# A hybrid attention and gating layer: output weights and gating result kept in memory as high and low parts

## The chip, the cores and the metric

One core of a Trainium2 chip runs the whole layer. The metric is the device time of one launch in microseconds (us), as the median of several runs. The core's engines work side by side, each through its own queue in order: TensorE (PE, with its weight loads PEld), VectorE (DVE), ScalarE (ACT), GpSimd (POOL), and SyncE (SP), which here issues every DMA.

## What is computed

The input x (2048 tokens by 1024) goes through one projection. Eight attention heads and a gating unit use its result, both results are joined (1024 wide) and go through one output projection, and a layer norm with a scaled residual ends it. Cut to what matters here:

```python
proj = jnp.einsum('bsd,de->bse', h, w_in)
attn = _causal_attention(qf, kf, val).reshape(b, s, MLA_WIDTH)
out_a = attn * jax.nn.silu(z_a)
sgu = u * sv.reshape(b, s, G_WIDTH)          # u, v: gelu; sv: causal mix of v
out_b = sgu * jax.nn.silu(z_b)
merged = jnp.concatenate([out_a, out_b], axis=-1)
y = jnp.einsum('bse,ed->bsd', merged, w_out)
h = _layernorm(DN_ALPHA * h + y, ln_g, ln_b)
```

## The kernel before

**Precision.** A float32 product is made of three matmuls on numbers in the format fp32r. Each operand is split into a high part (ACT copies it into an fp32r tile) and a low part (DVE subtracts the high part from the operand); the product is high by high, high by low and low by high. So an operand that comes from memory costs a load into one of five `raw` buffers, one copy on ACT and one subtraction on DVE. All the subtractions go through a helper and carry its line, L98.

**Input stage** (up to some 515 us). Two halves of 1024 tokens. In each, blocks of features of `w_in` (c = 0 to 11, 128 columns each; `feat`) are multiplied for two tiles of 512 tokens (L859). Blocks 4 to 7 give u, so their gelu times the gate (ACT L970, POOL L978) is the gating result out_b, stored whole as `ob_d` (L992). After block 7 come the latents (L853), whose weights w_c go into ring slots 0 to 3 as soon as block 5 has left them. The activations of a gate block hold a `tmp` buffer, of which there are ten.

**Attention** (some 515 to 1050 us). Eight heads, each of four query tiles of 512, with 3, 7, 11 and 15 units: 36 units in a head. A unit is three score matmuls (L422 to L424), exponent and high part on ACT (L432, L438), the low part on DVE (`pl`, L98), a row sum on POOL (L453) and two matmuls with the values (L466, L467). Beside a head run the row maxima for the next (L349 on PE, L356 and L359 on DVE). A finished tile needs a fold on ACT and DVE, a sum on POOL, and in odd heads two products on POOL (L600) whose factors come over DMA: the tile's row sums are gathered (`lc`, L578), inverted, stored (`r_d`, L584), loaded broadcast (`rb`, L596), and the product is stored as `oa_d` (L606).

**Output projection.** Its operands are the eight blocks of `w_out` (k = 0 to 7) and, for each tile st of 512 tokens, eight blocks of the joined result: k = 0 to 3 from `oa_d`, k = 4 to 7 from `ob_d`. `weights` (L1398, L1401) loads and splits the 16 half blocks of weights, `merged` (L1413, L1416) the eight blocks of tile 0, all in heads 6 and 7. Tile 0 is then multiplied inside head 7 (`block`, eight of them, 24 matmuls each, L1381 into bank_c), tile 1 is loaded at the end of head 7, tiles 2 and 3 by `load_m` (L1367) while the tile before is multiplied (L1381 into bank_a).

**What sets the order.** `op` records each step with engine, length, rank and dependencies; `issue` plays them through with booked lengths (`LENGTH`, `LAG`; 2.4 us for the landing of a DMA) and writes each engine's queue in that order. Among steps that can start, the lowest rank wins; a step that could start earlier fills a gap. Two engines are kept apart (`pair`) where the step says so; the subtractions of `weights` and `merged` do not say it. `YSTART` and the `spread` calls at the end of `y_jobs` set the ranks of the output projection's steps in units.

## Time and profile before

| | before |
|---|---|
| median of 3 runs | 1188.37 us (1185.0 to 1190.04) |
| the profiled execution | 1188.45 us, its span 1186.4 us |
| PE busy | 1148.7 us of the span (97%) |
| DVE, ACT, POOL busy | 851.1, 614.8, 505.3 us |
| PE's share of the chain that ended last | 83% |
| moved by DMA | 117.09 MB |

The profile is of one execution. Busy time is a share over stages with different limits, so the stretches are read one by one: the input stage to about 515 us, heads 0 to 5 to 872.7 us, head 6 to 936.2 us, head 7 to about 1032 us, the rest of the output projection to the end. "Granted clock" (PEclk) is TensorE's clock as a share of full speed.

### The profile page before, as it was taken

The numbers are of one execution on the slowest core, as the hardware profiler recorded it, in microseconds if no ns is written. First come the engines' busy times: TensorE is split into PE (matmuls) and PEld (weight loads), VectorE is DVE, ScalarE is ACT, GpSimd is POOL, SyncE is SP. The second block draws the span as 40 slices with busy tenths as digits, with TensorE's granted clock in tenths as the row PEclk, the third lists the DMA queues.
The fourth block names the chain that finished last, engine by engine and source line by source line (L and its number), as shares of the span: only waits on it lengthen the run. The fifth ranks groups of instructions, "written<-read, shape, count | busy, mean of one in ns | idle before, by whom it ended". The sixth has DMA issues, their size and how long they took to land.

```text
span 1186.4 us, 17288 instructions
## 1 busy us (share of the span) xinstructions
PE 1148.7 (97%) x5497; PEld 942.0 (79%) x5497; DVE 851.1 (72%) x2022; ACT 614.8 (52%) x1203; POOL 505.3 (43%) x482
## 2 busy tenths in 40 slices
PE   8999999999999999999999999999999879999997
PEld 6888899878888997777777777877777558878886
DVE  4777455446743386568899889898989973459866
ACT  5552413246433124248888788887888663432000
POOL 1112210101022121118799989987999774510000
PEclk9999999999999999989999999999999889999999
DMA  7311414365124216330031112111322234276431
GB/s 248 97 54 46 137 39 147 110 200 164 41 59 117 80 49 194 131 112 28 27 90 55 45 48 70 54 46 40 79 77 72 72 89 142 80 224 229 160 133 63
DMA packets 76075, 117.09 MB, mean 99 GB/s; under 512 B 18304, under 2 KB 22416, under 8 KB 75792
## 3 DMA queue, kind: packets, MB, share of 16 engines
q1 hardware_dynamic: 75984, 115.99, 31.4%
q8 instruction: 43, 0.70, 0.3%
q14 instruction: 48, 0.39, 0.1%
HBM read 79.58 MB, written 36.24 MB: 98 GB/s over the span
## 4 chain that ended last, share of the span: by engine, by line
PE 83%; DVE 5%; DMA 4%; ACT 3%; POOL 3%; issue 2%; SPq 0%; DVEq 0%; POOLq 0%; ACTq 0%
PE bank_a L859 22%; PE bank_a L853 13%; PE bank_a L1381 11%; PE bank_c L349 5%; PE bank_a L422 4%; PE bank_b L467 4%; PE bank_b L466 4%; PE bank_a L423 4%; PE bank_a L424 4%; PE bank_c L1381 3%; PE bank_a L1186 2%; PE bank_b L930 2%; POOL acc L453 1%; DVE pl L98 1%; PE bank_c L311 1%
## 5 line engine op out<-in xcount | busy, mean ns | idle before, releaser
L859 PE MATMUL bank_a<-xbuf,ring 128*128 128x512 f32 x1152 | 278.8, 394 | 6.3 <-ACT xbuf L709 5.5
L859 PEld LDWEIGHTS bank_a<-xbuf,ring 128*128 128x128 f32 x1152 | 215.1, 189 | 51.0 <-ACT xbuf L709 6.1
L432 ACT ACTIVATE bank_a<-bank_a 128x512 f32<-128x512 f32 (+1 forms) x288 | 163.6, 575 | 82.2 <-PE bank_a L424 47.2
L453 POOL TENSOR_TENSOR acc<-acc,xbuf 128x512 f32<-128x512 f32 (+2 forms) x168 | 194.9, 1160 | 21.3 <-ACT xbuf L438 12.6
L853 PE MATMUL bank_a<-ring,xbuf 128*128 128x512 f32 (+1 forms) x768 | 169.9, 373 | 0.0
L853 PEld LDWEIGHTS bank_a<-ring,xbuf 128*128 128x128 f32 x768 | 142.9, 189 | 16.5
L98 DVE TENSOR_TENSOR ring<-raw,ring 128x512 fp32r<-128x512 f32 (+1 forms) x88 | 70.9, 816 | 100.2 <-ACT ring L709 92.7
L359 DVE TENSOR_REDUCE mxt<-bank_c 128x1 f32<-128x512 f32 (+1 forms) x192 | 126.9, 666 | 18.4 <-PE bank_c L349 16.6
L98 DVE TENSOR_TENSOR pl<-bank_a,xbuf 128x512 fp32r<-128x512 f32 (+1 forms) x192 | 125.9, 661 | 18.2 <-ACT xbuf L438 16.8
L467 PE MATMUL bank_b<-pl,xbuf 128*128 128x512 f32 (+1 forms) x320 | 119.2, 376 | 9.4 <-ACT bsb L528 6.4
L438 ACT CAST xbuf<-bank_a 128x512 fp32r<-128x512 f32 (+1 forms) x192 | 107.6, 574 | 7.6 <-ACT bank_a L432 0.4
L453 POOL TENSOR_TENSOR acc<-acc,ph 128x512 f32<-128x512 f32 (+1 forms) x72 | 86.0, 1195 | 11.4 <-ACT ph L438 7.4
L466 PE MATMUL bank_b<-xbuf 128*128 128x512 f32 (+2 forms) x216 | 81.3, 380 | 0.0
L467 PEld LDWEIGHTS bank_b<-pl,xbuf 128*128 128x128 f32 x320 | 61.8, 193 | 20.0 <-ACT bsb L528 6.9
L98 DVE TENSOR_TENSOR pl<-bank_a,ph 128x512 fp32r<-128x512 f32 x96 | 65.1, 685 | 16.6 <-ACT ph L438 15.9
L356 DVE CUSTOM_DVE_ANT_0 bank_c<-bank_c,maskq 128x256 f32<-128x256 f32 (+3 forms) x128 | 65.7, 519 | 8.0 <-PE bank_c L349 6.9
L709 ACT CAST ring<-raw 128x512 fp32r<-128x512 f32 (+1 forms) x72 | 42.2, 601 | 55.9 <-PE bank_a L859 31.7
L970 ACT ACTIVATE act_t<-bank_a 128x512 f32<-128x512 f32 x40 | 23.9, 598 | 85.5 <-PE bank_a L859 85.1
L422 PE MATMUL bank_a<-xbuf,ring 97*128 97x512 f32 (+2 forms) x160 | 61.7, 386 | 3.6 <-DVE pl L98 3.3
L98 POOL TENSOR_TENSOR held<-qrt 128x128 f32<-128x128 f32 x16 | 7.4, 460 | 133.2 <-DVE qrt L1144 123.5
L422 PE MATMUL bank_a<-q,ring 97*128 97x512 f32 (+2 forms) x160 | 62.3, 389 | 0.3 <-DVE pl L98 0.3
L349 PE MATMUL bank_c<-ring,xbuf 96*128 96x512 f32 (+2 forms) x160 | 60.9, 390 | 1.0 <-DVE mxt L359 0.6
...
## 6 DMA issues: line engine op xcount, KB each, us to landing
...
```

What stands on the lines that cost most here:

```text
L98: eng.tensor_tensor(out=out_, in0=a, in1=b, op=ALU.subtract)
L349: pe.matmul(st_["x"][:, :hi - lo], qs_(h, 0)[0:DQK, qb * P:end], kslot(h)[0:DQK, 0, lo:hi], start=True, stop=True)
L359: dve.tensor_reduce(out=mx[h][:, qb, c:c + 1], in_=xps, axis=AX.X, op=ALU.max)
L422: pe.matmul(o_, k_[0:DQK + 1, 0, js], q_[0][0:DQK + 1, qs], start=True, stop=False)
L432: act.activation(out=o_, in_=o_, func=AF.Exp, scale=SCALE)
L438: act.copy(out=un["ph"][:, c0:512], in_=un["x"][:, c0:512])
L453: pool.tensor_tensor(out=t_["acc"][:, cs], in0=t_["acc"][:, cs], in1=f(p_), op=ALU.add)
L466: pe.matmul(a_ps[:, cs], va, un["ph"][:, ps], start=first, stop=last)
L467: pe.matmul(b_ps[:, cs], vb, un["pl"][:, ps], start=first, stop=last and qt > 0)
L853: pe.matmul(dst[:, :n], a[:, k, js], b[:, 0:4, k, 0:cols], start=(k == 0 and i == 0), stop=(k == KT - 1 and i == 2))
L859: pe.matmul(dst, a[:, slot, k, :], b[:, k, :], start=(k == 0 and i == 0), stop=(k == KT - 1 and i == 2))
L1381: pe.matmul(y, mo(st, k, a)[:, js], wo(k, w)[:, ns], start=(k == kord(st)[0] and i == 0), stop=(k == kord(st)[-1] and i == 2))
```

## The change

The weights of the output projection are split in the input stage. While feature blocks 4 to 7 are multiplied, `keep_wo` loads a half block of `w_out`, copies its high part (ACT), subtracts (DVE) and stores both parts in the new `wo_d` (16 half blocks over the two halves). The gating result is split there too: `feat` copies its high part into a second `tmp` buffer, subtracts, and stores both parts in `ob_d`, which is now twice as large. In heads 6 and 7 `weights` is a plain transfer of 512 KB into the ring, `ckv` or `wo` tile for each block and part (16 of them), and `merged` for k = 4 to 7 two transfers of 256 KB. `load_m` does likewise for tiles 2 and 3. Blocks k = 0 to 3 are still split on arrival, their subtraction now kept apart from POOL's steps. `YSTART` goes from 6 to 14, and two ranges of ranks end later.

```diff
-    UNITS, YSTART, VLATE = 36, 6, 9
+    UNITS, YSTART, VLATE = 36, 14, 9
+    WO_AT = 4
-    ob_d = dram.tile([4, P, S], F32, name="ob_d")
+    ob_d = dram.tile([2, 4, P, S], F32, name="ob_d")
+    wo_d = dram.tile([2, KT, P, D], F32, name="wo_d")
...
+        def keep_wo(k, n, rank):
+            ns = slice(n * 512, (n + 1) * 512)
+            st_ = {}
+            def load():
+                st_["raw"] = raw2k([P, 512])
+                sp.dma_start(out=st_["raw"], in_=w_out[k * P:(k + 1) * P, ns])
+            def high():
+                st_["h"] = tp.tile([P, 512], F32R, name="wo_h", tag="held2k", bufs=2)
+                act.copy(out=st_["h"], in_=st_["raw"])
+            def store(c):
+                sp.dma_start(out=wo_d[c, k, :, ns], in_=st_["raw"] if c else f(st_["h"]))
+            d_ = op("sp", 256, rank, load)
+            h_ = op("act", 512, rank, high, [d_])
+            l_ = op("dve", 512, rank, lambda: sub(dve, st_["raw"].bitcast(F32R), st_["raw"], f(st_["h"])), [h_],
+                    times=1.1, pair=True)
+            s_ = [op("sp", 256, rank, lambda c=c: store(c), [o]) for c, o in enumerate((h_, l_))]
+            d_.takes.append(("raw", [s_[1]]))
+            h_.takes.append(("held", [s_[0], l_]))
...
-            if c >= 4:
-                dst = ob_d[c - 4, :, ss] if c < 8 else za_d[c - 8, :, ss]
-                o = op("sp", 256, rank, lambda: sp.dma_start(out=dst, in_=st_["t"]), [o])
+            if 4 <= c < 8:
+                h_ = op("act", 512, rank + 2, lambda: act.copy(out=st_["h"], in_=st_["t"]), [o])
+                l_ = op("dve", 512, rank + 2, lambda: sub(dve, st_["t"].bitcast(F32R), st_["t"], f(st_["h"])), [h_],
+                        times=1.1, pair=True)
+                s_ = op("sp", 256, rank + 2, lambda: sp.dma_start(out=ob_d[0, c - 4, :, ss], in_=f(st_["h"])), [h_])
+                o = op("sp", 256, rank + 2, lambda: sp.dma_start(out=ob_d[1, c - 4, :, ss], in_=st_["t"]), [l_])
+                a_.takes.append(("tmp", [s_, l_]))
...
+                    if WO_AT <= c < WO_AT + 4:
+                        keep_wo(4 * hf + c - WO_AT, s2, T)
...
+        if k > 3:
+            for c in range(2):
+                sp.dma_start(out=f(mo(st, k, c)), in_=ob_d[c, k - 4, :, ss])
+            return
...
-        def weights(k, n, r):
+        def weights(k, c, r):
...
             def load():
-                if k in (2, 3) and n == 0:
+                if k in (2, 3) and c == 0:
                     wo8_alloc(k - 2)
-                st_["raw"] = raw2k([P, 512])
-                sp.dma_start(out=st_["raw"], in_=w_out[k * P:(k + 1) * P, ns])
-            d_ = op("sp", 0, r, load, [done["s"][H - 2, 0 if k > 3 else NT - 1]])
-            h_ = op("act", 512, r, lambda: act.copy(out=wo(k, 0)[:, ns], in_=st_["raw"]), [d_, *(old if k > 3 else idle)])
-            l_ = op("dve", 512, r, lambda: sub(dve, wo(k, 1)[:, ns], st_["raw"], f(wo(k, 0)[:, ns])), [h_])
+                sp.dma_start(out=f(wo(k, c)), in_=wo_d[c, k])
+            ready.setdefault(k, []).append(op("sp", 512, r, load, old if k > 3 else idle))
...
+            def parts():
...
+                for c in range(2):
+                    sp.dma_start(out=f(mo(st, k, c)), in_=ob_d[c, k - 4, :, st * 512:(st + 1) * 512])
+            if k > 3:
+                ready.setdefault(k, []).append(op("sp", 512, r, parts, deps, times=1.2))
+                return
-            l_ = op("dve", 512, r, lambda: sub(dve, mo(st, k, 1), st_["raw"], f(mo(st, k, 0))), [h_])
+            l_ = op("dve", 512, r, lambda: sub(dve, mo(st, k, 1), st_["raw"], f(mo(st, k, 0))), [h_], pair=True)
...
-        for ks, lo, hi in ((KORD[:4], base - UNITS + 18, base), (KORD[4:], base + 2, base + 14)):
+        for ks, lo, hi in ((KORD[:4], base - UNITS + 18, base), (KORD[4:], base + 2, base + 24)):
...
-               base + YSTART + 6, base + UNITS + 6)
+               base + YSTART + 6, base + UNITS + 14)
```

Since `issue` writes the queues anew, three places matter.

**DVE, near the end of head 6.** `mxt` is the maximum over a row, `oa_9669` and `ckv` take a block of tile 0 and a block of weights. Before:

```order
L98 TENSOR_TENSOR pl<-bank_a,xbuf 128x512
L98 TENSOR_TENSOR oa_9669<-raw,oa_9669 128x512
L372 TENSOR_REDUCE mrow<-mxt 128x4
L98 TENSOR_TENSOR pl<-bank_a,xbuf 128x512
L98 TENSOR_TENSOR ckv<-raw,ckv 128x512
L98 TENSOR_TENSOR pl<-bank_a,xbuf 128x512
L359 TENSOR_REDUCE mxt<-bank_c 128x1
```

The same place now (the helper's line is L101 there):

```order
L101 TENSOR_TENSOR pl<-bank_a,xbuf 128x512
L375 TENSOR_REDUCE mrow<-mxt 128x4
L362 TENSOR_REDUCE mxt<-bank_c 128x1
L101 TENSOR_TENSOR pl<-bank_a,xbuf 128x512 x2
L362 TENSOR_REDUCE mxt<-bank_c 128x1
```

The two subtractions are gone, and nothing stands between the units' own.

**PE, in head 7, where tile 0 of the output projection begins.** Before, behind the scores of head 7's 22nd unit:

```order
L424 MATMUL bank_a<-xbuf,ring 128x512
L1381 MATMUL bank_c<-ring,xbuf 128x512 x3
L1381 MATMUL bank_c<-ring,oa_9669 128x512 x3
L1381 MATMUL bank_c<-ring,xbuf 128x512 x3
L1381 MATMUL bank_c<-ring,oa_9669 128x512 x3
L1381 MATMUL bank_c<-ckv,oa_9669 128x512 x12
L1381 MATMUL bank_c<-ring,xbuf 128x512 x12
```

Now, behind the scores of the 25th unit (L427 is the third of the score matmuls, L469 and L470 are those with the values):

```order
L427 MATMUL bank_a<-xbuf,ring 128x512
L469 MATMUL bank_b<-xbuf 128x256
L470 MATMUL bank_b<-pl,xbuf 128x256
L469 MATMUL bank_b<-xbuf 128x256
L470 MATMUL bank_b<-pl,xbuf 128x256
L1415 MATMUL bank_c<-ring,xbuf 128x512 x3
L1415 MATMUL bank_c<-ring,oa_9520 128x512 x3
L1415 MATMUL bank_c<-ring,xbuf 128x512 x3
L1415 MATMUL bank_c<-ring,oa_9520 128x512 x3
L1415 MATMUL bank_c<-ckv,oa_9520 128x512 x12
L1415 MATMUL bank_c<-ring,xbuf 128x512 x6
```

The projection starts three units later. Of its 192 matmuls 96 now stand behind the last scores of head 7, where 42 stood.

**SP, in the first half of the input stage, around the loads of w_c.** Before:

```order
L702 DMA raw<-in_w_feat_dram 128x512 x8
L702 DMA raw<-in_w_c_dram 128x416 x5
L992 DMA ob_d<-act_t 128x512 x2
L702 DMA raw<-in_w_c_dram 128x416 x3
```

Now, from the store of the second tile of feature block 5 on:

```order
L1024 DMA ob_d<-act_h 128x512
L1025 DMA ob_d<-act_t 128x512
L743 DMA wo_d<-raw 128x512
L705 DMA raw<-in_w_c_dram 128x416 x2
L736 DMA raw<-in_w_out_dram 128x512
L705 DMA raw<-in_w_c_dram 128x416
L1024 DMA ob_d<-act_h 128x512
L1025 DMA ob_d<-act_t 128x512
L743 DMA wo_d<-wo_h 128x512
L743 DMA wo_d<-raw 128x512
L705 DMA raw<-in_w_c_dram 128x416 x4
```

One store of a gating tile pair and one load of w_c follow these. The loads of w_c now stand behind stores that wait for ACT, POOL and DVE.

## Rows read from the trace of the kernel before

**Rows 1.** The page: busy time, share of the span and instructions by engine.
```profile
PE 1148.7 (97%) x5497; PEld 942.0 (79%) x5497; DVE 851.1 (72%) x2022; ACT 614.8 (52%) x1203; POOL 505.3 (43%) x482
```

**Rows 2.** Busy time by stretch: input stage, head 2, head 6, head 7, the rest.
```profile
core 0: us, PE busy (x) PEld busy (x) DVE busy (x) ACT busy (x) POOL busy (x), PEclk, DMA share, GB/s
96.00:156.00 60.00, 60.00 (x270) 50.24 (x269) 37.41 (x85) 20.30 (x35) 15.90 (x12) 1.00 0.30 92
342.00:402.00 60.00, 60.00 (x270) 50.36 (x269) 15.81 (x20) 18.21 (x33) 15.70 (x12) 1.00 0.29 86
...
636.60:693.70 57.10, 55.92 (x275) 44.14 (x274) 51.26 (x112) 45.87 (x88) 53.12 (x47) 1.00 0.19 52
872.70:936.20 63.50, 59.50 (x273) 45.01 (x272) 60.78 (x117) 51.71 (x103) 57.66 (x48) 0.95 0.30 84
936.20:981.00 44.80, 34.84 (x154) 25.62 (x153) 36.68 (x59) 31.55 (x62) 30.70 (x24) 0.92 0.32 89
981.00:1046.00 65.00, 65.00 (x293) 53.19 (x293) 26.70 (x41) 22.80 (x40) 31.42 (x26) 1.00 0.37 117
1046.00:1058.00 12.00, 9.77 (x40) 6.67 (x39) 4.86 (x9) 3.21 (x6) 1.14 (x1) 1.00 0.80 229
```

**Rows 3.** Groups of instructions, 872.7 to 981 us: busy us, mean ns | idle before.
```profile
L453 POOL TENSOR_TENSOR acc<-acc,xbuf 128x512 f32<-128x512 f32 (+2 forms) x33 | 40.6, 1230 | 3.5 <-ACT xbuf L438 1.7
...
L98 DVE TENSOR_TENSOR pl<-bank_a,xbuf 128x512 fp32r<-128x512 f32 (+1 forms) x38 | 24.8, 656 | 2.1 <-ACT xbuf L438 1.9
...
L98 DVE TENSOR_TENSOR ring<-raw,ring 128x512 fp32r<-128x512 f32 x8 | 9.3, 1164 | 0.0
...
L98 DVE TENSOR_TENSOR oa<-raw,oa 128x512 fp32r<-128x512 f32 x3 | 6.8, 2259 | 0.0
...
L1401 ACT CAST wo<-raw 128x512 fp32r<-128x512 f32 x4 | 2.5, 618 | 5.3 <-DMA raw<-in_w_out_dram 5.3
```

**Rows 4.** In order of time (start, us): a long subtraction, two stops of PE.
```profile
917.49 4.34 DVE L98 TENSOR_TENSOR oa<-raw,oa 128x512 fp32r<-128x512 f32 x1
...
949.54 0.50 PE L422 MATMUL bank_a<-xbuf,ring 97*128 97x512 f32 x1 [2.28 <-DVE pl L98]
...
971.20 0.80 PE L467 MATMUL bank_b<-pl,xbuf 128*128 128x512 f32 x1 [6.43 <-ACT bsb L528]
```

**Rows 5.** Chain that ended last (start, us, what), 963 to 979 us.
```profile
963.34 6.68 DMA raw<-in_w_out_dram
...
973.70 0.43 PE bank_b L466
...
978.35 0.23 PE bank_b L466
```

**Rows 6.** Busy time in shorter stretches, columns as in rows 2.
```profile
962.00:968.00 6.00, 2.77 (x13) 1.78 (x11) 2.29 (x5) 2.13 (x4) 3.05 (x3) 1.00 0.96 256
...
962.00:980.00 18.00, 11.57 (x45) 8.98 (x44) 10.04 (x16) 11.33 (x23) 13.38 (x11) 0.81 0.48 133
```

**Rows 7.** Chain that ended last: DMA steps of a tile's row sums.
```profile
654.77 2.70 DMA r_d<-lc
...
731.74 4.20 DMA rb<-r_d
```

**Rows 8.** Between head 7 and tile 1, in order of time: SP's queue.
```profile
1046.08 0.32 SPq L1446 DMA_DIRECT2D h_d<-raw  x1
```

**Rows 9.** Groups of the input stage, 342 to 402 us: splits on DVE and ACT.
```profile
L98 DVE TENSOR_TENSOR ring<-raw,ring 128x416 fp32r<-128x416 f32 (+1 forms) x14 | 13.3, 951 | 45.7 <-ACT ring L709 45.6
...
L709 ACT CAST ring<-raw 128x416 fp32r<-128x416 f32 (+1 forms) x14 | 8.0, 572 | 12.2 <-PE bank_a L859 9.2 <-DMA raw<-in_w_feat_dram 2.9
```

**Rows 10.** PE in order of time: the first latents of the first half.
```profile
149.99 0.73 PE L853 MATMUL bank_a<-ring,xbuf 128*128 128x416 f32 x3
```

**Rows 11.** Waits over the whole run: total us, times, longest.
```profile
SPq L992 <- POOL act_t L978: 64.6, 16, 18.9
...
POOL opair L600 <- DMA raw<-za_d: 20.0, 4, 14.3
```

More of the change, by code (lines that the diff above doesn't have):

```diff
@@ L724, in load_wide @@
                      lambda: wr_l[:, 0:4, k, :n], eng, [("w", s, k) for s in range(4)], home=home)
+        def keep_wo(k, n, rank):
[16 more added lines that the diff above has]
+            h_.takes.append(("held", [s_[0], l_]))
+            writes(s_, [("wo", k, n)])
         def load_x(st, k, eng, rank):
@@ L969, in silu @@
                 st_["t"] = held() if c < 2 else tmp([P, 512], name="act_t")
+                if 4 <= c < 8:
+                    st_["h"] = tmp([P, 512], F32R, name="act_h")
                 act.activation(out=st_["t"], in_=st_["x"], func=AF.Gelu if 4 <= c < 8 else AF.Silu)
@@ L989, in feat @@
                 o = a_
-            if c >= 4:
-                dst = ob_d[c - 4, :, ss] if c < 8 else za_d[c - 8, :, ss]
-                o = op("sp", 256, rank, lambda: sp.dma_start(out=dst, in_=st_["t"]), [o])
+            if 4 <= c < 8:
+                h_ = op("act", 512, rank + 2, lambda: act.copy(out=st_["h"], in_=st_["t"]), [o])
[4 more added lines that the diff above has]
+                a_.takes.append(("tmp", [s_, l_]))
+            elif c >= 8:
+                o = op("sp", 256, rank, lambda: sp.dma_start(out=za_d[c - 8, :, ss], in_=st_["t"]), [o])
             a_.takes.append(("held" if c < 2 else "tmp", [o]))
@@ L1347, in wo @@
         return ring[:, i * 2048 + c * 1024:i * 2048 + (c + 1) * 1024]
-    def load_wo(k):
-        for n in range(2):
-            ns = slice(n * 512, (n + 1) * 512)
-            raw = raw2k([P, 512])
-            sp.dma_start(out=raw, in_=w_out[k * P:(k + 1) * P, ns])
-            act.copy(out=wo(k, 0)[:, ns], in_=raw)
-            sub(dve, wo(k, 1)[:, ns], raw, f(wo(k, 0)[:, ns]))
     def mo(st, k, c):
@@ L1364, in load_m @@
     def load_m(st, k):
+        ss = slice(st * 512, (st + 1) * 512)
+        if k > 3:
+            for c in range(2):
+                sp.dma_start(out=f(mo(st, k, c)), in_=ob_d[c, k - 4, :, ss])
+            return
         raw = raw2k([P, 512])
-        src = oa_d if k < 4 else ob_d
-        sp.dma_start(out=raw, in_=src[k % 4, :, st * 512:(st + 1) * 512])
+        sp.dma_start(out=raw, in_=oa_d[k, :, ss])
         act.copy(out=mo(st, k, 0), in_=raw)
@@ L1412, in load @@
                 st_["raw"] = raw2k([P, 512])
-                sp.dma_start(out=st_["raw"], in_=(oa_d if k < 4 else ob_d)[k % 4, :, st * 512:(st + 1) * 512])
-            d_ = op("sp", 0, r, load, [*deps, done["oa"][k, st] if k < 4 else None])
+                sp.dma_start(out=st_["raw"], in_=oa_d[k, :, st * 512:(st + 1) * 512])
+            def parts():
+                if "oa12" not in att:
+                    out_alloc()
+                for c in range(2):
[3 more added lines that the diff above has]
+                return
+            d_ = op("sp", 0, r, load, [*deps, done["oa"][k, st]])
             h_ = op("act", 512, r, lambda: act.copy(out=mo(st, k, 0), in_=st_["raw"]), [d_])
-            l_ = op("dve", 512, r, lambda: sub(dve, mo(st, k, 1), st_["raw"], f(mo(st, k, 0))), [h_])
+            l_ = op("dve", 512, r, lambda: sub(dve, mo(st, k, 1), st_["raw"], f(mo(st, k, 0))), [h_], pair=True)
             d_.takes.append(("raw", [l_]))
@@ L1450, in y_jobs @@
         base = UNITS * (H - 1)
-        for ks, lo, hi in ((KORD[:4], base - UNITS + 18, base), (KORD[4:], base + 2, base + 14)):
+        for ks, lo, hi in ((KORD[:4], base - UNITS + 18, base), (KORD[4:], base + 2, base + 24)):
             jobs = []
             for k in ks:
-                jobs += [(1, lambda r, k=k, n=n: weights(k, n, r)) for n in range(2)]
+                jobs += [(1, lambda r, k=k, c=c: weights(k, c, r)) for c in range(2)]
                 jobs.append((1, lambda r, k=k: merged(0, k, r, old)))
```

4 lines of the change are left out of this document (removed).

## Prediction

> **What bounds the kernel now.** I read the page's busy times first: PE is busy for 1148.7 us of 1186.4 [rows 1], so the 37.7 us in which it stands still, and the stretches in which its clock is down, are all that a change which leaves PE its work can win. Then the stretches [rows 2]. In the two parts of the input stage that the change loads, PE never stops. In head 2 it is busy for 55.92 of 57.1 us. In head 6, which has the same 36 units, it needs 63.5 us, stands still for 4.0 and has a mean clock of 0.95. From head 7's start to the first matmul of the output projection (981 us) it stands still for 9.96 of 44.8 us at a mean clock of 0.92. From there the projection's matmuls fill every gap, up to 1046 us, and around the change to tile 1 PE loses another 2.23 us.
>
> Then I asked what ends these gaps. In head 6 DVE is busy for 60.78 of 63.5 us (96%, against 90% in head 2) [rows 2]. The splitting has filled it, and at far more than its price: a low part whose operand lies in PSUM (`pl`) takes 0.66 us, one with both operands in SBUF 1.16 us into `ring` and 2.26 us into `oa` [rows 3], one of them 4.34 us [rows 4], while POOL is busy for 91% of that stretch. A unit's own `pl` queues behind, and PE stops for it (2.28 us, the wait on DVE in rows 4). The longest stop, 6.43 us, is put down to ACT's copy `bsb` [rows 4]; but ACT had four copies of `wo` ahead of it, and these had waited 5.3 us for their loads [rows 3], one of which took 6.68 us [rows 5]. So ACT, in order, stood before a DMA, and PE behind ACT. After that stop a matmul takes 0.43 us instead of 0.23 [rows 5]: the granted clock had fallen to the lower of its levels, 1.2 of 2.4 GHz (mean 0.81 over these 18 us [rows 6]).
>
> **Head 6.** Of the 24 copies and 24 subtractions in these heads, 20 of each go (16 for weights, 4 for tile 0's k = 4 to 7). Ten of the subtractions stand in head 6. What is left of the head is what head 2 does, with transfers beside it that no engine waits for in between. So I give it head 2's 57.1 us: 63.5 − 57.1 = 6.4 us won. From both sides: 0, if the time came from something else than the splits, and 63.5 − 55.9 = 7.6, if PE never stopped.
>
> The Trainium skill (GPSIMD Engine Reference, Key points) says that POOL shares its SBUF interfaces with VectorE and contends with VectorE instructions that have two SBUF inputs. The spread from 0.66 to 4.34 us agrees. The rule speaks against this change too: the 32 new subtractions also have two SBUF inputs. At 2.26 us each they would add 36 us of DVE to each half of the input stage instead of 15, and in the first half 37.4 + 36 is more than the 60 us that are there; the sum below goes by 0.95 us.
>
> **Head 7 up to the projection.** 44.8 us now. Of PE's 34.84 busy us, 12 matmuls ran at 0.43 instead of 0.23 us, some 2.3 us; its work at full clock is 32.5. All that could be won is 44.8 − 32.5 = 12.3. But the projection now begins three units later, so three more units (five matmuls of 0.23 us each, 3.5 us in all, moved and not added) must run without its cover. For these 25 units I count PE 32.5 + 3.5 = 36.0 us; POOL 30.7 + 3 row sums of 1.23 us [rows 3] = 34.4; ACT and DVE, less 13 splits, some 27 each. PE is last by only 1.6 us, so the next one is POOL. And the projection needs block k = 3 of tile 0, which goes through head 7's first tile: gather, store, broadcast, product, store, load. Its planner books 2.4 us for a landing; the rows have 2.70 and 4.20 [rows 7]. With four such steps late by 1 us each I leave 4 us of standstill: **8.3 us won**, between 12.3 (no wait left) and 0 (the chain is that late).
>
> **Change to tile 1.** Before, only 42 matmuls stood behind the last scores; SP waited at 1046.08 us to store a block of tile 0 before it could load tile 1 [rows 8], and PE stopped. Now 96 stand there (22 us at 0.23), and the loads of k = 1 to 3 follow the stores of the fifth and sixth block, the second of which ends half way, some 12 us before they are needed. A load of 4 us, a copy and a subtraction fit. Against it stand 2 MB of `ob_d` in place of 1 in the same queues, 8 us at the 256 GB/s of rows 6. I take 1.5 of the 2.23 us; bounds 2.2 and, where the queues are late, −2. Tiles 2 and 3 lose 8 splits on engines that PE does not wait for, and carry 2 MB more over 88 us: nothing.
>
> **The input stage.** Each half gets 16 splits: 16 subtractions of 0.95 and 16 copies of 0.57 us [rows 9], 15 us of DVE and 9 of ACT, and 32 more transfers of 256 KB (8 loads and 24 stores). DVE goes from 37.4 to 53 of 60 us in the first half and from 15.8 to 31 in the second, ACT to 29 and 27 [rows 2]; 8.4 MB more in 60 us lift the 92 GB/s to some 230, under the 256 that rows 6 show. What hides it is that PE runs on 60 us of work whose operands are there. The queue is another matter. SP now stands before stores that wait for ACT, POOL and DVE, and the loads of w_c queue behind. The last of these waits, ahead of the eighth load, is for the second tile of block 6: PE ends it two chains of 24 matmuls (5.3 us each, by 270 in 60 us [rows 2]) before block 7's end at about 151 us, so at 140.5. Gelu, gate, copy and subtraction take some 3.3 us, an estimate from a copy (0.57, twice), a row sum of POOL (1.23) and a subtraction (0.95); the load 4, copy and subtraction 1.5: some 149.5 us. PE begins the latents at 149.99 us [rows 10] and reaches that eighth block some 21 matmuls later, at about 154.6. So 5 us are left. Cost within cover 0; I charge 1.5 us for the changed order around the latents, from −2 (the planner's new order happens to close a gap of the 2 us that the rest of the stage has) to +6.
>
> The Trainium skill (DMA: Bandwidth & Descriptors, on where the fixed cost goes) says that a DMA's fixed part of about 2 us is mostly the receipt of the write and heaviest towards HBM. The new stores would hold `raw` and `tmp` buffers that long, which speaks against the change; the rows have 2.70 us for the smallest store, in the range counted here.
>
> **The sum.** 6.4 + 8.3 + 1.5 − 1.5 = 14.7 us off the profiled execution's own 1188.45 us gives 1173.8. That execution lies 0.1 us above the median of its three runs, so the same figure stands for the median: **1173.7 us**, by itself between 1168 and 1181.
>
> **The rivals.**
> - *All stops go.* Nothing waits in head 7, the change to tile 1 is closed, the input stage costs nothing: 1188.4 − 6.4 − 12.3 − 2.2 = 1167.5. For it: POOL and ACT are below PE by the count above. Against it: only 1.6 us of margin.
> - *A new late item in head 7.* Eight transfers of 512 KB for k = 0 to 3 may start only when head 6's scores are done; 4 MB at 256 GB/s are 16 us, and the row sums' small steps share the queue. If tile 0's operands are complete 48 us after head 7's start instead of 36, nothing is won there: 1188.4 − 6.4 − 1.5 + 1.5 = 1182. For it: the load of 6.68 us in a crowded queue [rows 5]. Against it: these loads stood there before, with half the bytes but with splits behind them.
> - *POOL waits in order.* One wait of POOL for a gate load lasted 14.3 us [rows 11]. If the direct transfers push a factor of a product back by as much while no projection covers it, row sums, ACT and PE stand behind it and the gain is gone: 1188. Against it: raw buffers are freer now.
> - *Slower, by the queue of the input stage.* SP has waited up to 18.9 us for a gate product [rows 11]; before, w_c did not stand behind. If it does so now in each half, 18.9 − 5 = 14 us of PE's time are lost twice, and the gain stays: 1173.7 − 1.5 + 28 = 1200. It decides from 5 us of delay in w_c on, and exceeds the gain from 8 us over that in each half. For it: in the first half DVE is at 88%. Against it: that long wait lay where nothing was due.
>
> **How the numbers follow.** Forecast 0.60, all stops go 0.12, late item 0.12, POOL's wait 0.09, slower 0.07. A measurement of this kernel tells 0.5% (5.9 us) from no change, so faster means below 1182.4: 0.60 + 0.12 and half of the late item, 0.78; the same: the other half and POOL's wait, 0.15; slower 0.07. The range from 1167 to 1183 leaves out the last two cases and part of the first rival.
>
> **What would show it.** In the profile after: head 6 near 57 us with DVE at or under 90%, no subtraction above 1.5 us in it; the projection's first matmul near 971 us (981 + 3.5 + 1.5 − 6.4 − 8.3) in place of 981; no clock below 0.95 over head 7; PE without a stop at tile 1; PE at 60 of 60 us in the input stage's two stretches. It is wrong if head 6 stays above 60 us with DVE relieved, if PE stops before the latents, or if the stop at the projection's start is above 8 us.

## The result and the profile after

The changed kernel takes 1167.39 us (median of 4 runs, 1166.87 to 1170.33) against 1187.47 us of the kernel before on the same chip (4 runs, 1185.00 to 1190.04). The ratio is 0.984, with a 95% interval from 0.982 to 0.986: faster by 20 us (1.6%), where 14.7 were forecast. The profiled execution has a span of 1165.1 us, 21.3 less than before.

Page of the changed kernel, the row of busy times that answers to [rows 1]:

```profile
PE 1138.1 (98%) x5497; PEld 937.5 (80%) x5497; DVE 840.6 (72%) x2022; ACT 616.1 (53%) x1203; POOL 498.4 (43%) x482
```

Every engine runs as many instructions as before. DVE is busy for 10.5 us less and PE for 10.6 us less, although neither lost one: in both the same work took less time.

Busy time by stretch, columns as in [rows 2]: the two parts of the input stage, head 6, head 7 up to the projection, from there to tile 1, and the first 12 us of tile 1.

```profile
96.00:156.00 60.00, 60.00 (x269) 50.07 (x268) 39.08 (x88) 23.51 (x40) 16.40 (x12) 1.00 0.55 154
342.00:402.00 60.00, 60.00 (x268) 49.96 (x267) 22.38 (x31) 22.75 (x42) 14.42 (x11) 1.00 0.61 185
871.90:926.90 55.00, 54.77 (x274) 43.90 (x273) 50.46 (x112) 47.10 (x91) 52.06 (x47) 1.00 0.57 167
926.90:962.00 35.10, 33.69 (x168) 26.13 (x168) 26.05 (x45) 29.50 (x58) 29.35 (x25) 1.00 0.52 153
962.00:1026.40 64.40, 62.14 (x271) 50.03 (x270) 25.00 (x39) 20.66 (x37) 31.85 (x27) 0.97 0.55 160
1026.40:1038.40 12.00, 12.00 (x55) 9.93 (x54) 2.89 (x5) 0.00 (x0) 2.59 (x2) 1.00 0.72 210
```

Head 6 takes 55.0 us instead of 63.5, and PE is busy in 54.77 of them. Head 7 up to the projection takes 35.1 instead of 44.8 with three units more. The stop at tile 1 is gone. The stretch between is the only one that lost: before, PE was busy there without a gap; now it stands still for 2.3 us, at a mean clock of 0.97.

What PE waits for from 868 to 985 us (total us, times, longest), first before and then after:

```profile
PE bank_b L467 <- ACT bsb L528: 6.4, 1, 6.4
PE bank_a L422 <- DVE pl L98: 3.6, 5, 2.3
PE bank_b L467 <- DVE pl L98: 2.9, 1, 2.9
PE bank_c L349 <- DVE mxt L359: 0.6, 1, 0.6
```

```profile
PE bank_a L425 <- DVE pl L101: 1.4, 2, 0.9
PE bank_c L564 <- POOL accl L101: 1.3, 1, 1.3
PE bank_c L564 <- ACT acch L555: 1.0, 1, 1.0
PE bank_c L352 <- DVE mxt L359: 0.2, 1, 0.2
```

13.5 us of waits became 3.9. The long ones, for a `bsb` copy behind splits on ACT and for a `pl` behind splits on DVE [rows 4], are gone. Two new ones come from the end of a tile's row sums: POOL's sum, ACT's copy `acch`, POOL's rest `accl`. PE in order of time shows them, and what follows (start, us, and in brackets the idle time):

```profile
974.51 0.39 PE L470 MATMUL bank_b<-pl,xbuf 128*128 128x512 f32 x1
975.87 0.51 PE L564 MATMUL bank_c<-acch,zo 128*128 128x512 f32 x1 [0.96 <-ACT acch L555]
977.67 0.51 PE L564 MATMUL bank_c<-accl,zo 128*128 128x512 f32 x1 [1.30 <-POOL accl L101]
978.01 0.58 PE L425 MATMUL bank_a<-xbuf,ring 97*128 97x512 f32 x1
...
979.24 0.63 PE L469 MATMUL bank_b<-ph,xbuf 128*128 128x512 f32 x1
...
982.81 0.40 PE L469 MATMUL bank_b<-xbuf 128*128 128x512 f32 x1
```

Behind the two stops a matmul's record is 0.63 us long instead of 0.39 (the records of neighbours overlap; in the chain the same matmuls stand at 0.43 and 0.23). So the granted clock had fallen to the lower level here too, for some 3.5 us: the starts are 0.43 us apart up to 981.6 us, and from 977.6 to 983.0 us its mean is 0.68.

By stages, from the first matmul of each:

| stage, span us | before | after | difference | forecast |
|---|---|---|---|---|
| start to head 6 | 872.77 | 871.89 | −0.9 | +1.5 |
| head 6 | 63.45 | 55.05 | −8.4 | −6.4 |
| head 7 to the projection | 44.59 | 35.08 | −9.5 | 3.5 − 8.3 = −4.8 |
| projection's start to tile 1 | 63.47 | 64.35 | +0.9 | −3.5 |
| tile 1 to the end | 142.12 | 138.73 | −3.4 | −1.5 |
| sum | 1186.4 | 1165.1 | −21.3 | −14.7 |

The 3.5 us are the three units that moved from behind the projection's start to ahead of it. The first row compares an execution whose clock fell at the start of head 0 with one whose clock did not; that is worth some 3 us, and the last section has it.

### The profile page after: what moved, and what is told of

The parts are those of the page before. It is cut to its first block, busy times and chain, and to the rows that moved or that the text cites. A ratio compares the mean times of both kernels' runs of the same rounds, so it can differ in the third digit from the quotient of the medians.

```text
span 1165.1 us, 17412 instructions
## 1 busy us (share of the span) xinstructions
PE 1138.1 (98%) x5497; PEld 937.5 (80%) x5497; DVE 840.6 (72%) x2022; ACT 616.1 (53%) x1203; POOL 498.4 (43%) x482
## 4 chain that ended last, share of the span: by engine, by line
PE 84%; DVE 4%; POOL 4%; ACT 3%; DMA 2%; issue 2%; SPq 0%; DVEq 0%; POOLq 0%; ACTq 0%
PE bank_a L887 21%; PE bank_a L881 13%; PE bank_a L1415 11%; PE bank_c L352 5%; PE bank_b L469 4%; PE bank_a L425 4%; PE bank_b L470 4%; PE bank_a L426 4%; PE bank_a L427 4%; PE bank_c L1415 3%; POOL acc L456 2%; PE bank_a L1222 2%; PE bank_b L958 2%; DMA rb<-r_d 1%; PE bank_c L314 1%
## 5 line engine op out<-in xcount | busy, mean ns | idle before, releaser
L456 POOL TENSOR_TENSOR acc<-acc,xbuf 128x512 f32<-128x512 f32 (+2 forms) x168 | 192.2, 1145 | 15.2 <-ACT xbuf L441 6.6
L101 DVE TENSOR_TENSOR pl<-bank_a,xbuf 128x512 fp32r<-128x512 f32 (+1 forms) x192 | 126.1, 662 | 29.2 <-ACT xbuf L441 26.1
L470 PE MATMUL bank_b<-pl,xbuf 128*128 128x512 f32 (+1 forms) x320 | 116.9, 369 | 0.0
L441 ACT CAST xbuf<-bank_a 128x512 fp32r<-128x512 f32 (+1 forms) x192 | 107.7, 572 | 10.4 <-POOL acc L456 2.4
L101 DVE TENSOR_TENSOR ring<-raw,ring 128x512 fp32r<-128x512 f32 (+1 forms) x80 | 58.0, 739 | 51.2 <-ACT ring L712 46.5
L469 PE MATMUL bank_b<-xbuf 128*128 128x512 f32 (+2 forms) x216 | 80.6, 376 | 0.0
L101 DVE TENSOR_TENSOR pl<-bank_a,ph 128x512 fp32r<-128x512 f32 x96 | 65.1, 684 | 11.9 <-ACT ph L441 11.2
L470 PEld LDWEIGHTS bank_b<-pl,xbuf 128*128 128x128 f32 x320 | 60.9, 190 | 8.3 <-DVE opair L534 0.3
L101 POOL TENSOR_TENSOR held<-qrt 128x128 f32<-128x128 f32 x16 | 7.4, 461 | 128.2 <-DVE qrt L1180 98.2
```

Of the source, the lines that this page charges most:

```text
L101: eng.tensor_tensor(out=out_, in0=a, in1=b, op=ALU.subtract)
L441: act.copy(out=un["ph"][:, c0:512], in_=un["x"][:, c0:512])
L456: pool.tensor_tensor(out=t_["acc"][:, cs], in0=t_["acc"][:, cs], in1=f(p_), op=ALU.add)
L469: pe.matmul(a_ps[:, cs], va, un["ph"][:, ps], start=first, stop=last)
L470: pe.matmul(b_ps[:, cs], vb, un["pl"][:, ps], start=first, stop=last and qt > 0)
```

## The experiments

The theory (A) was the prediction's: the splits in heads 6 and 7 hold PE up, on DVE because they are long and on ACT because they wait for loads. Rivals were that the new ranks (`YSTART` and the two ranges) did it, that the subtractions were long for another reason than POOL, and that the gain of one part hides a loss of another. Ratios are to the kernel before on the same chip, with their 95% intervals.

### Each part alone

Run `e1_wo`: the weights' part and the ranks, with the gating result left as it was.

```diff
 # the changed kernel, but:
-                s_ = op("sp", 256, rank + 2, lambda: sp.dma_start(out=ob_d[0, c - 4, :, ss], in_=f(st_["h"])), [h_])
-                o = op("sp", 256, rank + 2, lambda: sp.dma_start(out=ob_d[1, c - 4, :, ss], in_=st_["t"]), [l_])
...
+                o = op("sp", 256, rank, lambda: sp.dma_start(out=dst, in_=st_["t"]), [o])
```

> The changed kernel with the gating result as before (stored whole, split on arrival): only the weights are split in the input stage. Theory A, the gain is the splitting time taken out of heads 6 and 7: 16 of the 20 splits stay away, the ones that ACT waited for included, so 14 to 18 us under the kernel before, 1170 to 1174 us. Rival B, the new ranks make the gain: 1167 to 1169, as the whole change. Rival C, the gating part (the subtractions into oa, 2.26 us each before) makes half of it: 1177 or more.

1174.44 us (1172.48 to 1175.93), ratio 0.9894 [0.9875, 0.9912]: 13.3 us won, just less than theory A said, and outside B and C.

Run `e2_gate`: the gating result's part and the ranks, with `weights` of the kernel before.

```diff
 # the changed kernel, but:
-                        keep_wo(4 * hf + c - WO_AT, s2, T)
...
-                sp.dma_start(out=f(wo(k, c)), in_=wo_d[c, k])
+            h_ = op("act", 512, r, lambda: act.copy(out=wo(k, 0)[:, ns], in_=st_["raw"]), [d_, *(old if k > 3 else idle)])
+            l_ = op("dve", 512, r, lambda: sub(dve, wo(k, 1)[:, ns], st_["raw"], f(wo(k, 0)[:, ns])), [h_])
```

> The changed kernel with the weights as before (loaded and split in heads 6 and 7): only the gating result is split in the input stage. Theory A: 4 of 20 splits are gone from the last two heads and ACT still waits for the weights' loads, so 3 to 7 us under the kernel before, 1181 to 1185 us. Rival B, new ranks: 1167 to 1172. Rival C: 1177 or less.

1180.13 us (1177.10 to 1181.32), ratio 0.9938 [0.9915, 0.9961]: 7.6 us won, a little more than theory A said, and short of B and C. The two parts give 13.3 + 7.6 = 20.9 us, and the whole change 20.1. Within the intervals, which reach some 2 us to either side, they add up. Head 6 and head 7 up to the projection in the two runs, columns as before, `e1_wo` first:

```profile
871.60:928.60 57.00, 55.73 (x275) 43.74 (x274) 53.31 (x115) 48.33 (x95) 52.59 (x46) 1.00 0.47 141
928.60:964.40 35.80, 33.81 (x165) 25.62 (x164) 29.35 (x47) 29.19 (x59) 30.19 (x26) 1.00 0.52 154
```

```profile
873.50:931.30 57.80, 56.01 (x274) 43.23 (x273) 56.23 (x116) 49.77 (x99) 54.07 (x46) 1.00 0.39 117
931.30:977.70 46.40, 39.64 (x184) 30.41 (x183) 39.89 (x62) 37.90 (x75) 38.48 (x30) 0.93 0.32 85
```

Either part alone brings head 6 down to 57 to 58 us. Head 7 comes down only without the weights' splits; with them (`e2_gate`) it keeps 6.8 us without a matmul and the mean clock of 0.93.

### The ranks

Run `e3_ranks_back`: the whole change with the ranks of the kernel before.

```diff
-    UNITS, YSTART, VLATE = 36, 14, 9
+    UNITS, YSTART, VLATE = 36, 6, 9
...
-        for ks, lo, hi in ((KORD[:4], base - UNITS + 18, base), (KORD[4:], base + 2, base + 24)):
+        for ks, lo, hi in ((KORD[:4], base - UNITS + 18, base), (KORD[4:], base + 2, base + 14)):
...
-               base + YSTART + 6, base + UNITS + 14)
+               base + YSTART + 6, base + UNITS + 6)
```

> The changed kernel with the ranks of the kernel before (YSTART 6, the two ranges end as before). Theory A: the ranks matter little, 1167 to 1171 us. Rival B, the later start of the projection makes the gain: 1178 or more.

1168.19 us (1167.53 to 1169.07), ratio 0.9842 [0.9828, 0.9857]. The interval covers the whole change's 0.984: the ranks give nothing that can be measured. The rival falls. (From head 6's first score matmul to the end its profiled execution takes 291.3 us, the changed kernel's 293.2.)

### What the input stage pays

Run `e4_no_input`: the whole change without the splits in the input stage. Left out: splitting weights and gating result; the transfers read other numbers of the same size from `qn_d`.

```diff
-                    if WO_AT <= c < WO_AT + 4:
-                        keep_wo(4 * hf + c - WO_AT, s2, T)
...
-                h_ = op("act", 512, rank + 2, lambda: act.copy(out=st_["h"], in_=st_["t"]), [o])
...
-                sp.dma_start(out=f(wo(k, c)), in_=wo_d[c, k])
+                sp.dma_start(out=f(wo(k, c)), in_=qn_d[c, k % 4, :, (k // 4) * 1024:(k // 4) * 1024 + 1024])
```

> The changed kernel without any split in the input stage: the plain transfers of the last two heads and of tiles 1 to 3 read other tensors of the same sizes in memory (parts of qn_d), so that the projection multiplies other numbers; the gating result is stored whole and not read. It measures what the input stage pays. Theory A, the splits there are hidden: 0 to 2 us faster than the changed kernel, 1165 to 1168 us. Rival D, they cost a good part of the gain: 1162 or less.

1165.12 us (1164.87 to 1165.25), ratio 0.9816 [0.9801, 0.9831]. Against the changed kernel's 1167.39 that is 2.3 us by the medians. It is not the input stage's share alone: in the profiled execution of this run the clock fell at the start of head 0, in the changed kernel's it did not (last section). The traces tell the share ahead of that place. Head 0's first score matmul, in this run and in the changed kernel:

```profile
515.50 0.42 PE L425 MATMUL bank_a<-q,ring 97*128 97x384 f32 x1
```

```profile
517.29 0.42 PE L425 MATMUL bank_a<-q,ring 97*128 97x384 f32 x1
```

That is 1.8 us. In the five profiled executions with the changed kernel's input stage it stands at 516.67 to 517.29 us, in the five with the input stage of before at 514.20 to 515.17: 2.4 us later on the mean.

### Which half of a split costs

Run `e6_no_sub`: the kernel before, without the 16 subtractions of the weights. Left out: their low parts, which a plain transfer fills with other numbers.

```diff
-            l_ = op("dve", 512, r, lambda: sub(dve, wo(k, 1)[:, ns], st_["raw"], f(wo(k, 0)[:, ns])), [h_])
+            l_ = op("sp", 256, r, lambda: sp.dma_start(out=f(wo(k, 1)[:, ns]), in_=qn_d[1, k % 4, :, (k // 4) * 1024 + n * 512:(k // 4) * 1024 + (n + 1) * 512]), [d_, *(old if k > 3 else idle)])
```

> The kernel before without the subtractions of the 16 weight splits: each low part is a plain transfer of other numbers of the same size from memory (qn_d), so the projection multiplies other numbers; the loads of w_out and the copies on ACT stay. Theory A1, DVE's subtractions are most of the loss: half or more of the 13 us that the weights' part was worth, 1175 to 1181 us. Rival A3, ACT in order before a load is most of it: 1182 to 1187.

1176.60 us (1173.90 to 1178.63), ratio 0.9909 [0.9891, 0.9926]: 10.4 us won.

Run `e7_no_copy`: the kernel before, without the 16 copies of the weights on ACT. Left out: their high parts, in the same manner.

```diff
-            h_ = op("act", 512, r, lambda: act.copy(out=wo(k, 0)[:, ns], in_=st_["raw"]), [d_, *(old if k > 3 else idle)])
+            h_ = op("sp", 256, r, lambda: sp.dma_start(out=f(wo(k, 0)[:, ns]), in_=qn_d[0, k % 4, :, (k // 4) * 1024 + n * 512:(k // 4) * 1024 + (n + 1) * 512]), [d_, *(old if k > 3 else idle)])
```

> The kernel before without the copies on ACT of the 16 weight splits: each high part is a plain transfer of other numbers of the same size from memory (qn_d); the loads of w_out and the subtractions on DVE stay. Theory A1: the subtractions still fill DVE, 1181 to 1187 us. Rival A3, ACT in order before a load is most of the loss: 1175 to 1180.

1183.19 us (1177.64 to 1185.00), ratio 0.9963 [0.9941, 0.9984]: 3.9 us won. Both runs also order their queues anew, so the two are not exact halves; but without DVE's part of the weights' splits by far more is won. In the profile of `e6_no_sub` the gain lies in head 7: head 6 is no shorter, with seven of the eight subtractions left in it, and head 7 up to the projection takes 30.3 us:

```profile
870.20:935.10 64.90, 58.31 (x275) 44.46 (x274) 60.25 (x118) 51.54 (x104) 55.54 (x48) 0.97 0.42 128
935.10:965.40 30.30, 29.51 (x146) 22.18 (x145) 20.75 (x38) 28.60 (x58) 24.48 (x22) 1.00 0.57 186
```

PE's stop for `bsb` is gone in it too, although all 16 copies and their loads stay; in its new order the four copies of `wo` wait for no load. In `e7_no_copy` that stop is gone as well, and PE waits for DVE instead.

### Why the subtractions are long

Run `e5_apart`: the kernel before, with its planner told to keep the subtractions of heads 6 and 7 apart from POOL's steps.

```diff
-... [h_])
+... [h_], pair=True)
```

(in the subtractions of `weights` and of `merged`.)

> The kernel before; only its planner now keeps the subtractions of the last two heads' splits apart from POOL's steps (pair=True), as it does for those of the input stage. Theory A1, what made them expensive is that they run beside POOL: no subtraction above 1.5 us is left or few are, the 24 fall from 28.7 us in all to some 18, and the time to 1179 to 1184 us. Rival A2, their number and the copies make the time, not their length: 1186 to 1190.

1185.26 us (1181.22 to 1190.02), ratio 0.9985 [0.9968, 1.0003]: no difference that can be measured, and a time between the two forecasts. It doesn't speak against the theory, for the subtractions didn't get shorter; the plan kept them apart, the chip did not. Two rows in order of time, DVE and POOL:

```profile
951.03 2.36 DVE L98 TENSOR_TENSOR ring<-raw,ring 128x512 fp32r<-128x512 f32 x2
...
954.75 1.44 DVE L98 TENSOR_TENSOR xbuf<-raw,xbuf 128x512 fp32r<-128x512 f32 x1
```

```profile
951.09 1.75 POOL L453 TENSOR_TENSOR acc<-acc,ph 128x512 f32<-128x512 f32 x1
952.92 1.63 POOL L534 TENSOR_TENSOR opair<-opair,bsb 64x512 f32<-64x512 f32 x1
954.63 1.01 POOL L453 TENSOR_TENSOR acc<-acc,xbuf 128x384 f32<-128x384 f32 x1
```

The subtraction at 954.75 runs beside a row sum, and the two from 951.03 (2.36 us together) beside a row sum and the fold behind it. With 24 subtractions at a mean of 1.22 us (29.4 us in all, by the groups of the run) DVE had as much to do as before. So this run decides nothing.

Run `e9_small_sums` tests it from POOL's side. It is the kernel before, with the same order of the work on every engine; in heads 6 and 7 POOL's row sums (but for the first of a tile) take 32 columns. Left out: the rest of those sums.

```diff
-                        pool.tensor_tensor(out=t_["acc"][:, cs], in0=t_["acc"][:, cs], in1=f(p_), op=ALU.add)
+                        pool.tensor_tensor(out=t_["acc"][:, cs][:, :32 if h > 5 else None], in0=t_["acc"][:, cs][:, :32 if h > 5 else None], in1=f(p_)[:, :32 if h > 5 else None], op=ALU.add)
```

> The kernel before, in the same order on every engine, but in heads 6 and 7 POOL's row sums after the first of a tile add 32 columns instead of 128 to 512 (left out: the rest of those sums, so these heads' normalization is not the reference's). The splits stay where they are. Theory A, that the splits of these heads are long because they run beside POOL's row sums: the 24 subtractions that read `raw` take some 17 to 19 us in all, 0.7 to 0.8 each, instead of 28.7 us, none above 1.5; head 6 falls from 63.5 to 57 to 60 us, and the time by 8 to 13 us to 1174 to 1179 us. Rival B, that they are long because of the transfers beside them or for their buffers: the subtractions stay at 27 us or more in all with some above 2 us; the time falls by 5 us at most, by what POOL itself no longer delays.

1177.78 us (1174.27 to 1181.53), ratio 0.9929 [0.9903, 0.9954]: 8.3 us won. The subtractions that read `raw`, 868 to 985 us (min/median/max in ns; first and last start), before:

```profile
L98 DVE TENSOR_TENSOR ring<-raw,ring x8: 675/924/3009, 903.6 to 960.8; 128x512 fp32r<-128x512 f32 x8
L98 DVE TENSOR_TENSOR xbuf<-raw,xbuf x5: 681/981/1336, 911.2 to 979.6; 128x512 fp32r<-128x512 f32 x5
L98 DVE TENSOR_TENSOR ckv<-raw,ckv x4: 677/978/1556, 922.4 to 936.3; 128x512 fp32r<-128x512 f32 x4
...
L98 DVE TENSOR_TENSOR oa<-raw,oa x3: 683/1753/4341, 917.5 to 938.5; 128x512 fp32r<-128x512 f32 x3
```

and with the small row sums:

```profile
L98 DVE TENSOR_TENSOR ring<-raw,ring x8: 661/762/3012, 900.0 to 949.7; 128x512 fp32r<-128x512 f32 x8
L98 DVE TENSOR_TENSOR xbuf<-raw,xbuf x5: 670/689/693, 907.4 to 966.6; 128x512 fp32r<-128x512 f32 x5
L98 DVE TENSOR_TENSOR ckv<-raw,ckv x4: 683/687/715, 915.1 to 925.8; 128x512 fp32r<-128x512 f32 x4
...
L98 DVE TENSOR_TENSOR oa<-raw,oa x3: 682/687/944, 913.5 to 927.9; 128x512 fp32r<-128x512 f32 x3
```

The same instructions fall to medians of 0.69 to 0.76 us once POOL works less beside them. By the groups' busy times the 24 took 28.7 us before and 20.4 us here (8.9 + 3.4 + 2.8 + 3.0 + 2.3), where 24 of 0.69 are 16.6 us; so POOL's row sums account for 8.3 of the 12.1 us above that. That is less of a fall than the 17 to 19 us expected: one of 3.01 us stayed, beside two of POOL's steps that were not shortened (a fold at 934.92 and a tile's first sum at 936.52). The transfers beside them stayed (a DMA share of 0.32 in head 6 against 0.30), so rival B falls. The Trainium skill (GPSIMD Engine Reference, Key points) has POOL contend with VectorE instructions that have two SBUF inputs; the two profiles agree, with 0.69 us beside little POOL work and up to 4.34 us beside its sums. One by one the records of the kernel before, `e5_apart` and `e9_small_sums` say the same: of the 72 subtractions, the 13 with no POOL instruction beside them took 0.67 to 0.69 us, and all above 0.70 had one. But some that had one took 0.66 to 0.70 as well, so a step of POOL beside it can make a subtraction long and need not.

Head 6 and head 7 of this run by stretch, columns as before, and then PE's waits from 868 to 985 us:

```profile
869.00:925.70 56.70, 56.57 (x273) 43.20 (x272) 54.17 (x117) 50.66 (x102) 30.93 (x48) 1.00 0.32 94
925.70:967.80 42.10, 33.20 (x153) 24.62 (x152) 35.16 (x59) 31.96 (x63) 18.56 (x24) 0.92 0.31 89
```

```profile
PE bank_b L467 <- ACT bsb L528: 5.5, 1, 5.5
PE bank_a L422 <- DVE pl L98: 3.3, 4, 2.3
```

This tells the two heads apart. Head 6 falls to 56.7 us with PE at 56.57, all splits still in it: there the price was DVE's time beside POOL. DVE's share is 96% as before, but its 54.17 us are now less than PE's 56.57, where its 60.78 were more than PE's 59.50 [rows 2]. In head 7 the stop of 5.5 us for `bsb` and the clock of 0.92 stay, in the same order of the queues: ACT still stands with four copies of `wo` that wait for their loads. Short subtractions alone don't remove that; taking the splits away does, and so did the other order of `e6_no_sub`. Which of order, loads and copies it takes is not separated here.

### What is left behind the projection's start

Run `e10_after_small_sums`: the changed kernel with the same small row sums (left out: as above).

> The changed kernel with the same shortening of POOL's row sums in heads 6 and 7 (left out: as in the run before). It asks what POOL still costs once the splits are gone. Theory A, that POOL is the next late engine in head 7 and its `accl` stops PE behind the projection's start: that stop of 1.3 us and the lower clock behind it (64.4 us from the projection's start to tile 1, PE 62.1 busy) go, the stretch takes 60 to 62 us and the time 1162 to 1165 us, 2 to 5 us under the changed kernel. Rival B, that what PE loses there comes from the order or from the transfers: stretch and time stay within 1.5 us of the changed kernel's 64.4 and 1167.4 us.

1163.07 us (1161.59 to 1165.29), ratio 0.9806 [0.9786, 0.9826]: 4.3 us under the changed kernel. From the projection's start to tile 1:

```profile
963.70:1023.70 60.00, 60.00 (x271) 48.94 (x270) 25.02 (x39) 20.93 (x37) 14.69 (x27) 1.00 0.55 172
```

Without long row sums PE does not stop there, and the clock stays up: 60.0 us instead of 64.4. POOL is the next late engine. (By the ratios the two kernels' intervals overlap a little; the stretch is the clearer witness.)

Run `e8_not_apart`: the changed kernel with `pair=True` taken off the subtractions of blocks 0 to 3.

```diff
-            l_ = op("dve", 512, r, lambda: sub(dve, mo(st, k, 1), st_["raw"], f(mo(st, k, 0))), [h_], pair=True)
+            l_ = op("dve", 512, r, lambda: sub(dve, mo(st, k, 1), st_["raw"], f(mo(st, k, 0))), [h_])
```

> The changed kernel without the mark that keeps the subtractions of blocks 0 to 3 apart from POOL. Theory A1, a subtraction beside POOL is long: one or two of over 2 us come back, 1168 to 1172 us. Rival A2: 1167, no difference.

1170.53 us (1169.21 to 1170.77), ratio 0.9857 [0.9842, 0.9871]. By the medians it is 3 us slower than the changed kernel, as theory A1 said, but not for its reason. None of its four subtractions takes more than 1.26 us, and head 6, up to which its instructions are the changed kernel's, begins at 875.00 us instead of 871.89: the 3 us lie ahead of it, in the fall of the clock at head 0 (last section). From there to the end it takes 294.0 us against 293.2; its PE waits for POOL's `accl` for 2.8 us instead of 1.3. So the mark's worth is not shown.

Two attempts to better the changed kernel. `e11_wo_at_2` has the weights' splits two feature blocks earlier (`WO_AT = 2`), `e12_ystart_10` the projection's blocks from unit 10 (`YSTART = 10`).

```diff
 # e11_wo_at_2
-    WO_AT = 4
+    WO_AT = 2
...
 # e12_ystart_10
-    UNITS, YSTART, VLATE = 36, 14, 9
+    UNITS, YSTART, VLATE = 36, 10, 9
```

> The changed kernel with the weights' splits two feature blocks earlier (WO_AT 2 instead of 4), so that in half of the blocks they do not coincide with the splits of the gating result. An attempt to get back some of the 2.3 us that the input stage's splits cost. If that cost is DVE and the queues being crowded in blocks 4 to 7: 1165.5 to 1167 us. If it is the latents' place or the sum of the work: within 1 us of the changed kernel's 1167.4.

1167.99 us (1166.93 to 1168.40), ratio 0.9845 [0.9827, 0.9862]: nothing won by the median. But its profiled execution had the fall of the clock at head 0, and ahead of that it was faster: head 0's first score matmul stands at 515.34 us, where the changed kernel's input stage gives 516.67 to 517.29. So by one trace the place of the weights' splits is worth 1.3 to 2.0 us, which the median doesn't show.

> The changed kernel with the projection's blocks ranked from unit 10 instead of 14 of head 7. More projection matmuls stand in the last part of head 7 as cover and fewer behind its last scores. If the loss of some 4 us between the projection's start and tile 1 is a lack of cover: 1164 to 1166.5 us. If it is POOL's lateness, which the order of PE's fillers does not change: 1166.5 to 1169 us.

1169.46 us (1168.38 to 1172.42), ratio 0.9862 [0.9842, 0.9882]: not better by the median. In its profile the stop for `accl` is gone, so cover does close that stop. From head 6 to the end it takes 291.8 us against 293.2 of the changed kernel; but head 6 begins at 875.33 us instead of 871.89 after equal instructions, for here too the clock fell at head 0. So the median may hide a gain of some 1.4 us.

## Why the prediction held, point by point

The time lies within the range and at its low end. The two largest terms were too small, and two small stages came out with the other sign. Some 3 us of what was won beyond the forecast may be luck: the clock fell at the start of head 0 in the profiled execution before, from which the sum started, and not in the one after.

**Head 6: right in its mechanism, too small.** 8.4 us won where 6.4 were taken, and beyond the upper bound of 7.6. The bound took head 2 as the measure (55.92 busy); PE needs 54.77 us here, and stands still for 0.2. `e9_small_sums` shows the cause that was named: with short subtractions the same queues give 56.7 us. One sign was missed: DVE is busy for 50.46 of 55.0 us, 92% and not at most 90%.

**Head 7 up to the projection: the step that failed.** I won 8.3 of a ceiling of 12.3 us; measured are 9.5 us in the span, or 13.0 with the three units. Two numbers of that step were off. I left 4 us of standstill for the chain of a tile's row sums; it was 1.4 us. And I counted 36.0 us of work for PE; it was 33.69. The slow clock had been taken off rightly: from 936.2 to 962 us the clock was at 1.00, over 971.0 to 976.5 at 0.52, and then at 1.00 again. What was too much is, by an estimate, what stops add to busy time: in a row matmuls start 0.23 us apart, but the last one before a stop counts with its whole record of some 0.4 us. At the 0.20 us per record of the profile after (33.69 us for 168), the 154 before are 30.9 us and not 32.5. POOL was counted at 34.4 us and is busy for 29.35, ACT for 29.50; neither was late here by more than the 1.4 us. That POOL is the next engine shows only behind the projection's start (`e10_after_small_sums`). So the first matmul of the projection stands at 962.02 us, where some 971 were forecast.

**From there to tile 1: a cost at nothing that was not nothing.** I let the three units leave this stretch for 3.5 us, and counted the rest as full. It grew by 0.9, so 4.4 us were lost: 2.3 in two stops for `acch` and `accl`, and some 1.7 at the lower clock behind them (3.5 us at half speed). `e10_after_small_sums` shows that it is POOL: without long row sums the stretch takes 60.0 us, the 63.5 less 3.5 that I had counted.

**Change to tile 1: right, a little small.** PE is busy for 12.00 of 12 us where it lost 2.23 [rows 2]. The stage won 3.4 us. The remaining 1.2 are not at its end: the last 20 us have 12.3 us of PE in both profiles. They lie beside the stops, where busy time grows as in head 7: the 525 matmul records up to there take 118.70 busy us now and took 119.87 (in the first 20 us 90 records in 20.00, before 75 in 17.77).

**The input stage: within its bounds, hidden in the total.** PE runs 60 of 60 us in both stretches, as forecast. The latents begin at 151.12 us instead of 149.99 [rows 10], and a stop of 0.59 us for a low part of the queries stands at 192.52. Head 0's first score matmul comes some 2.4 us later than with the input stage of before, where 1.5 were charged, within −2 to +6. The stage table shows −0.9 to head 6 because of the clock at head 0. Against `e9_small_sums`, which has the instructions of before up to there and no fall of the clock either, head 6 begins 2.9 us later (871.89 and 869.00). The subtractions were cheaper than the 0.95 us that I took (of the weights' 16 the view has 15):

```profile
L101 DVE TENSOR_TENSOR act_t<-act_t,act_h x16: 674/683/693, 124.5 to 404.8; 128x512 fp32r<-128x512 f32 x16
L101 DVE TENSOR_TENSOR raw<-raw,wo_h x15: 676/691/1497, 92.3 to 382.4; 128x512 fp32r<-128x512 f32 x15
```

That is the point of the change: the same subtraction costs 0.68 us here, beside a POOL that is busy for a quarter of the time, and took 1.2 us on the mean in heads 6 and 7 (28.7 us for 24), where POOL was busy for 91% and 69% [rows 2].

**The rivals.** "All stops go" said 1167.5 us, and the time is that figure by chance: its stops in head 7 went, but the input stage did cost, POOL took some 4 us behind the projection's start, and the clock at head 0 gave some 3 back. The three others did not come: no wait of PE in the profile after is longer than 1.3 us between 868 and 985 us, and in the input stage PE is busy for 60 of 60 us.

## What to carry over

Before work is moved off a crowded stretch, look at what one instruction of it costs there and what the same form costs elsewhere in the trace: the difference is won as well, on top of the place. Work that an engine in order must do behind a load can cost that engine's consumers the load's delay (6.43 us here), so a split whose result is constant belongs where its operands are early. And when a stop goes, count the next engine's work in the stretch *behind* it as well: here POOL's lateness showed up there and cost 4.4 us. Last, compare two profiles from a common place on: what happened ahead of it, as the clock at head 0 here, then drops out.

## What the runs showed of the chip

**A drop of the clock that some executions have.** At the start of head 0 PE waits for operands in every profiled execution, and in nine of the 14 its clock falls, in five not. Columns as before, 510 to 545 us, of the kernel before and of `e9_small_sums`, whose instructions are the same up to head 6:

```profile
510.00:545.00 35.00, 32.54 (x160) 26.28 (x159) 24.36 (x60) 21.99 (x48) 11.50 (x12) 0.85 0.26 79
```

```profile
510.00:545.00 35.00, 31.66 (x176) 25.29 (x175) 27.23 (x66) 25.13 (x54) 14.07 (x13) 1.00 0.26 78
```

At a mean of 0.85 some 160 matmuls were done, at 1.00 176 in less busy time. Head 1 begins at 579.08 us in the one and at 575.82 in the other: some 3 us between executions of equal instructions. What the engine did before is the same in both: it waits 1.1 us, then 0.5 us, and the matmuls behind are slow in the one and not in the other:

```profile
519.26 1.65 PE L311 MATMUL bank_c<-wv,ckv 128*128 128x256 f32 x6 [0.51 <-ACT mst L380]
```

```profile
519.03 0.97 PE L311 MATMUL bank_c<-wv,ckv 128*128 128x256 f32 x6 [0.51 <-ACT mst L380]
```

Why is open.

The profile after has the clock at 1.00 there and the profile before at 0.85, which hides what the change costs in the input stage. The runs made from the changed kernel differ from it in the same way. `e3_ranks_back`, `e8_not_apart`, `e10_after_small_sums` and `e12_ystart_10` have its instructions up to head 6:

| profiled execution | clock, 510 to 545 us | head 0's first score matmul | head 6's first score matmul | from there to the end |
|---|---|---|---|---|
| before | 0.85 | 514.77 | 872.77 | 313.6 |
| `e9_small_sums` | 1.00 | 514.52 | 869.00 | 303.6 |
| after | 1.00 | 517.29 | 871.89 | 293.2 |
| `e3_ranks_back` | 0.85 | 516.97 | 874.47 | 291.3 |
| `e8_not_apart` | 0.85 | 517.10 | 875.00 | 294.0 |
| `e10_after_small_sums` | 0.85 | 516.67 | 874.49 | 287.9 |
| `e12_ystart_10` | 0.85 | 517.24 | 875.33 | 291.8 |
| `e11_wo_at_2` | 0.85 | 515.34 | 873.80 | 291.7 |
| `e4_no_input` | 0.85 | 515.50 | 872.96 | 290.5 |

So medians that differ by some 3 us or less don't rank these kernels; which of the executions without a profile had the fall can't be told. The whole change is far beyond it: from head 6's first score matmul to the end it won 20.4 us, and ahead of head 6 it paid 2 to 3. A difference of 3 us between two profiles of this kernel should be looked for at head 0 first.

**Keeping two engines apart in a plan does not keep them apart on the chip.** The mean subtraction took 1.20 us before and 1.22 us with the mark (`e5_apart`); only the longest fell, from 4.34 to 1.79 us.
